# Cosine-similarity attention on one core: the orders of all five engines searched anew, the first scores ahead of the second pair's norm sums, its log among the first exponentials

## The chip, the cores and the metric

The kernel runs on one core of a Trainium2 chip. The program gives each of a core's five engines its own instruction list, and the lists meet only at semaphores: PE (TensorE, matrix multiply; PEld is its loading of weights), ACT (ScalarE), DVE (VectorE), POOL (GpSimd) and SP, which here only issues DMAs. A second list of DMA issues, shown as ACTq, stands on ACT. In these traces an instruction that waits holds up all behind it in its list.

The metric is the device time of one execution in microseconds (us), the median over several runs. The profile is of one execution; its span is about 2 us shorter than the device time. Some executions of a kernel are slower than the rest; a run over 1.5% above the fastest of its kernel is called slow here.

## The reference

```python
# Q, K, V: (8, 12, 512, 64) float32; tau = 0.1
Q_norm = Q / (np.linalg.norm(Q, axis=-1, keepdims=True) + 1e-10)
K_norm = K / (np.linalg.norm(K, axis=-1, keepdims=True) + 1e-10)
scores = np.einsum('bhqd,bhkd->bhqk', Q_norm, K_norm) / tau
weights = np.exp(scores - np.max(scores, axis=-1, keepdims=True))
weights = weights / (np.sum(weights, axis=-1, keepdims=True) + 1e-10)
return np.einsum('bhqk,bhkd->bhqd', weights, V).astype(np.float32)
```

## The kernel before

The 96 heads are worked off as 48 pairs, numbered 0 to 47. The program is a list of named operations with their needs, and a table `ORDER` that gives the order on each engine. The names, with s the pair and w = 0 for Q, 1 for K:

| name | engine | what |
|---|---|---|
| `LD.s.w`, `LV.s`, `ST.s` | SP (three of the K loads: ACT) | load Q or K, load V, store the result |
| `SQ` | POOL, for the first pairs also ACT | squares of Q and K |
| `SSQ.s`, `RED.s.0` | PE, DVE | sums of squares: a matmul against the identity, then a small reduction |
| `LN`, `EX` | ACT | for pairs 0 and 1: norms by a log and an exp |
| `NEW.g.k` | DVE | for later pairs, in groups: norms by an integer first guess and two Newton steps |
| `SCL.s.w` | DVE (Q), POOL (K) | scale by the norms |
| `TR.s`, `EVA.s` | PE, DVE | transpose, copy the transpose out of PSUM, the memory PE writes to |
| `XT.s` | SP | for seven of the pairs K is transposed by a DMA instead |
| `SCO.s.c`, `EXP.s.c` | PE, ACT | scores and exponentials of the c-th quarter, 128 keys of both heads (pair 0: one head at a time, 512 wide) |
| `VC`, `PV`, `RCP`, `NRM` | POOL, PE, DVE | V to bf16, weighted sums, normalization |
| `warm`, `fill` | PE | dummy matmuls that keep PE's clock up in the head |

How an order becomes waits, and the operations that the argument touches (cuts are marked `...`):

```python
for e, ops in order.items():
    for o in ops:
        o.waits = [self.ops[n] for n in o.needs]
        if e in ("pe", "act"):       # needs on the same engine: no wait
            o.waits = [p for p in o.waits if p.eng != e or p.slot is not None or p.key in o.hard]
...
# pair s: loads; K of pairs 0, 1 and 2 is issued from ACT's queue
for w, x in ((0, Q), (1, K)):
    P.add(("LD", s, w), "act" if w and s < 3 else "sp", [...],
          lambda e, w=w, x=x: e.dma_start(out=qk[iq][:, w], in_=src(x, s)), ...)
...
# exponentials: two banks of scores, so SCO.c waits for EXP.(c-2)
P.add(("EXP", s, c), "act", before, lambda e, c=c, b=b: e.activation(
    out=et[iet][:, c, :, :], in_=sc_ps[:, 2 * b : 2 * b + 2, :], func=ACT.Exp, scale=inv_tau))
...
XT = {33, 39, 9, 45, 15, 21, 27}
FILL = (9, 16)
ORDER = {
    "sp": """ LD.0.0.0 LD.0.0.1 LD.1.0 LD.2.0 LV.0 LD.3.1 LD.3.0 LD.4.1 LD.4.0 LD.5.1 LD.5.0 ... """,
    "act": """ table LD.0.1 LD.1.1 LD.2.1 SQ.0.0.1 SQ.0.1 LN.0.0 EX.0.0 LN.0.1 SQ.1.1 EX.0.1 SQ.2.1
               LN.1 EX.1.0 EX.1.1 EXP.0.0.0 EXP.0.0.1 EXP.0.1.0 ... """,
    ...
```

## Time and profile before

| | before |
|---|---|
| device time, median of 3 runs | 194.69 us (194.19 to 194.87) |
| span of the profiled run | 192.28 us |
| first exponential starts | 9.59 us |
| start of the last exponential to the end | 4.88 us |
| median start-to-start of the 1024-wide exponentials | 0.904 us |
| starts later than 0.904 us after the one before, summed | 3.3 us |

The last two rows are worked out from the start times of the exponentials in the trace.

ACT is busy for 95% of the span and its exponentials follow one another with hardly any idle time. (Neighbours overlap, so the mean of 1135 ns is longer than their spacing.) What can shrink is what comes before the first exponential, gaps in their stream, and what follows the last. The head of ACT's timeline (start us, duration us, engine, line, operation, output<-input, count, [idle before <-what ended it]):

```profile
1.33 1.01 ACTq L379 DMA_DIRECT2D qk<-in_K_dram  x2
...
5.53 0.18 ACT L263 ACTIVATE ops<-xl 128x8 f32<-128x8 f32 x1
6.07 0.21 ACT L259 ACTIVATE xl<-xs 128x8 f32<-128x8 f32 x1 [0.36 <-DVE xs L304]
6.19 0.61 ACT L229 ACTIVATE sq<-qk 128x512 bf16<-128x512 f32 x1
6.71 0.19 ACT L263 ACTIVATE xr<-xl 128x8 f32<-128x8 f32 x1
7.38 0.63 ACT L229 ACTIVATE sq<-qk 128x512 bf16<-128x512 f32 x1 [0.49 <-DMA qk<-in_K_dram]
9.12 0.21 ACT L259 ACTIVATE xl<-xs 128x16 f32<-128x16 f32 x1 [1.11 <-DVE xs L253]
9.37 0.18 ACT L263 ACTIVATE ops<-xl 128x8 f32<-128x8 f32 x1
9.49 0.19 ACT L263 ACTIVATE xr<-xl 128x8 f32<-128x8 f32 x1
9.59 4.76 ACT L443 ACTIVATE et<-scps,xr 128x512 bf16<-128x512 f32 x8
14.21 6.77 ACT L453 ACTIVATE et<-scps 128x1024 bf16<-128x1024 f32 x7
```

The two loads at 1.33 are K of pairs 1 and 2. The square at 7.38 is `SQ.2.1`, of pair 2's K; it starts as that load lands, at 7.36. Then ACT idles 1.11 us for pair 1's norm sum, does pair 1's log and two exps (9.12 to 9.59), and only then begins pair 0's exponentials.

### The profile page before, as it was taken

The numbers are of one execution on the slowest core, as the hardware profiler recorded it, in microseconds if no ns is written. First come the engines' busy times: TensorE is split into PE (matmuls) and PEld (weight loads), VectorE is DVE, ScalarE is ACT, GpSimd is POOL, SyncE is SP. The second block draws the span as 40 slices with busy tenths as digits, with TensorE's granted clock in tenths as the row PEclk, the third lists the DMA queues.
The fourth block names the chain that finished last, engine by engine and source line by source line (L and its number), as shares of the span: only waits on it lengthen the run. The fifth ranks groups of instructions, "written<-read, shape, count | busy, mean of one in ns | idle before, by whom it ended". The sixth has DMA issues, their size and how long they took to land.

```text
span 192.3 us, 7111 instructions
## 1 busy us (share of the span) xinstructions
PE 179.5 (93%) x2944; PEld 117.6 (61%) x2944; DVE 148.3 (77%) x450; ACT 182.3 (95%) x210; POOL 161.8 (84%) x149
## 2 busy tenths in 40 slices
PE   7799999999998999999999899999999999999891
PEld 5466666656665565666666565666566656566560
DVE  1588887988888798868897887798888778976632
ACT  3599999999999999999999999999999999999990
POOL 4599899999999969999989988799999999927000
PEclk9999999999999999999999999999999999999998
DMA  5999999999999999989999999038799536650545
GB/s 185 360 349 349 352 336 321 373 251 344 341 376 303 374 364 332 314 251 310 364 346 339 285 376 387 16 88 254 242 254 356 130 109 197 193 136 3 182 148 165
DMA packets 56240, 51.71 MB, mean 269 GB/s; under 512 B 6928, under 2 KB 56208, under 8 KB 56208
## 3 DMA queue, kind: packets, MB, share of 16 engines
q1 hardware_dynamic: 55248, 50.41, 84.6%
q10 hardware_dynamic: 960, 0.85, 1.3%
q8 instruction: 23, 0.38, 0.9%
q14 instruction: 9, 0.07, 0.1%
HBM read 37.75 MB, written 12.58 MB: 262 GB/s over the span
## 4 chain that ended last, share of the span: by engine, by line
ACT 67%; POOL 15%; PE 8%; DMA 3%; DVE 2%; issue 2%; SPq 0%
ACT et L453 67%; POOL sq L231 8%; POOL qn L270 4%; DMA qk<-in_Q_dram 3%; POOL vb L458 3%; PE scps L431 2%; PE ops L469 2%; PE xps L246 2%; PE ops L218 1%; PE xps L277 1%; DVE ob L513 1%; PE nps L498 0%; SPq L294 0%; DVE ob L483 0%; POOL vb L212 0%
## 5 line engine op out<-in xcount | busy, mean ns | idle before, releaser
L453 ACT ACTIVATE et<-scps 128x1024 bf16<-128x1024 f32 x187 | 172.2, 1135 | 0.3
L231 POOL TENSOR_TENSOR sq<-qk 128x1024 bf16<-128x1024 f32 (+2 forms) x48 | 87.5, 1837 | 4.2 <-DMA qk<-in_Q_dram 4.2
L431 PE MATMUL scps<-qt 64*128 64x512 bf16 x384 | 74.7, 386 | 4.4 <-ACT et L453 2.4
L469 PEld LDWEIGHTS ops<-vb,et 128*128 128x128 bf16 x1504 | 53.4, 98 | 27.2 <-issue 22.2
L469 PE MATMUL ops<-vb,et 128*128 128x65 bf16 x1504 | 68.2, 194 | 0.6 <-DVE nps L341 0.4
L270 POOL TENSOR_TENSOR qn<-qk,rk 128x512 bf16<-128x512 f32 x44 | 45.6, 1046 | 10.2 <-DVE rk L346 10.2
L421 DVE COPY qt<-xps 128x1024 bf16<-128x1024 bf16 (+1 forms) x47 | 30.4, 647 | 3.7 <-PE xps L277 3.2
L483 DVE TENSOR_TENSOR ob<-ops,rd 128x512 f32<-128x512 f32 x47 | 32.4, 689 | 1.1
L270 DVE TENSOR_TENSOR qn<-qk,nps 128x512 bf16<-128x512 f32 x48 | 31.9, 680 | 0.3
L431 PEld LDWEIGHTS scps<-qt 64*128 64x128 bf16 x384 | 18.6, 92 | 20.3 <-ACT et L453 7.4
L458 POOL TENSOR_SCALAR vb<-vf 128x512 bf16<-128x512 f32 x48 | 29.7, 630 | 0.0
L277 PE MATMUL xps<-ident,qn 128*128 128x128 bf16 x352 | 27.9, 220 | 0.4 <-DVE qn L270 0.2
L246 PE MATMUL xps<-sq,ident 128*128 128x64 bf16 x624 | 24.9, 192 | 2.0 <-POOL sq L231 0.9
L277 PEld LDWEIGHTS xps<-ident,qn 128*128 128x128 bf16 x352 | 19.9, 98 | 10.4 <-issue 3.0
L246 PEld LDWEIGHTS xps<-sq,ident 128*128 128x128 bf16 x624 | 20.8, 97 | 8.9 <-issue 3.8
L481 DVE RECIPROCAL rd<-ops 128x8 f32<-128x8 f32 x47 | 9.7, 206 | 15.6 <-PE ops L469 15.2
L253 DVE TENSOR_REDUCE nps<-xps 128x16 f32<-128x64 f32 x38 | 8.8, 232 | 9.3 <-PE xps L246 8.9
L240 DVE TENSOR_REDUCE nps<-sq 128x8 f32<-128x512 bf16 x16 | 10.8, 684 | 0.0
L341 DVE TENSOR_TENSOR nps<-nps,ys 128x32 f32<-128x32 f32 (+1 forms) x48 | 9.3, 195 | 1.1
L342 DVE SCALAR_TENSOR_TENSOR nps<-nps,ys 128x32 f32<-128x32 f32 (+1 forms) x48 | 9.2, 193 | 1.0
L218 PE MATMUL scps<-warm_in 128*128 128x256 bf16 x28 | 5.8, 384 | 1.1 <-DVE warm_in L216 1.1
L218 PEld LDWEIGHTS scps<-warm_in 128*128 128x128 bf16 x28 | 3.7, 138 | 2.3 <-DVE warm_in L216 1.1
(42 smaller groups left out, 46.1 us busy)
## 6 DMA issues: line engine op xcount, KB each, us to landing
vf<-in_V_dram SPq DMA_DIRECT2D x48, 256.0 KB, 6.0
qk<-in_Q_dram SPq DMA_DIRECT2D x47, 256.0 KB, 6.0
out_dram<-ob SPq DMA_DIRECT2D x47, 256.0 KB, 5.3
qk<-in_K_dram SPq DMA_DIRECT2D x45, 256.0 KB, 6.0
qk<-in_K_dram ACTq DMA_DIRECT2D x3, 256.0 KB, 4.7
qk<-in_Q_dram SPq DMA_DIRECT2D x2, 128.0 KB, 2.7
out_dram<-ob SPq DMA_DIRECT2D x1, 128.0 KB, 2.3
qt<-qn SPq DMA_TRANSPOSE x7, 4.9
```

The source lines that it names most:

```text
L218: P.add(key, "pe", needs, lambda e: e.matmul(out=bank[:, 0:256], lhsT=warm_in[:, 0:128], rhs=warm_in[:, :], start=True, stop=True))
L231: emit = lambda e: e.tensor_tensor(out=b, in0=a, in1=a, op=ALU.mult)
L240: lambda e, w=w: e.tensor_reduce(out=dst(w), in_=sq[s % R_SQ][:, 8 * w : 8 * w + 8, :], axis=AX.X, op=ALU.add))
L246: last = e.matmul(out=x_ps[:, 0:64], lhsT=ident[:, :], rhs=sq[s % R_SQ][:, :, 4 * k : 4 * k + 4], start=(k == 0), stop=(k == 15))
L270: lambda e: e.tensor_tensor(out=qn[iqn][:, w].rearrange("p t h d -> p h t d"), in0=qk[iq][:, w].rearrange("p h (t d) -> p h t d", t=NT), i ...
L277: last = e.transpose(dst[:, i, :], qn[s % R_QN][:, b // NT, b % NT].rearrange("p h d -> p (h d)"), ident[:, :])
L421: lambda e: e.tensor_copy(out=qt[iqt][:, :].rearrange("p w t x -> p (w t) x")[:, 0:nb], in_=tb[:, 0:nb]))
L431: last = e.matmul(out=sc_ps[:, 2 * b + h, :], lhsT=qt[iqt][64 * h : 64 * h + 64, 1, c, :], rhs=qt[iqt][64 * h : 64 * h + 64, 0, :, :], sta ...
L453: lambda e, c=c, b=b: e.activation(out=et[iet][:, c, :, :], in_=sc_ps[:, 2 * b : 2 * b + 2, :], func=ACT.Exp, scale=inv_tau))
L458: lambda e: e.tensor_scalar(out=vb[:, iq, :, :, 0:DIM].rearrange("p c h d -> p h c d"), in0=vf[iv][:, :, :].rearrange("p h (c d) -> p h c ...
L469: last = e.matmul(out=o_ps[:, h, 65 * t : 65 * t + 65], lhsT=et[iet][:, c, h, 128 * t : 128 * t + 128], rhs=vb[:, iq, c, h, :], start=(c = ...
L483: lambda e: e.tensor_tensor(out=ob[io][:, :], in0=grid[:, :, :, 0:DIM], in1=rd[io][:, :].unsqueeze(3).to_broadcast([128, 2, NT, DIM]), op= ...
```

## The change

The intent: let pair 0's scores and first exponentials go ahead of pair 1's norm work, and find better orders for the rest by a search in an event model whose durations were fitted to the chip. No operation is added or taken away; the lists of all five engines are permuted. The diff, cut to what bears on the argument:

```diff
-        dummy(("fill", k), *((sc_ps[:, 3], ["wz"]) if k < FILL[0] else (o_ps[:, 0], [("EVA", 0, 1)])))
+        low = k < FILL[0]
+        dummy(("fill", k), sc_ps[:, 3] if low else o_ps[:, 0],
+              [("fill", k - 1) if k else ("warm", WARM - 1), "wz" if low else ("EVA", 0, 1)])
+    P.ops["SCO", 0, 1].needs.append(("fill", FILL[0] - 1))
+    P.ops["PV", 0, 0, 0].needs.append(("fill", sum(FILL) - 1))
 ...
     "pool":
-        one eye SQ.0.0.0 SCL.0.1 SQ.1.0 vone SQ.2.0 SCL.1.1 VC.0 SQ.3.0 ...
+        one eye SQ.0.0.0 SCL.0.1 vone SQ.1.0 SQ.2.0 VC.0 SCL.1.1 SQ.3.0 ...
     "dve":
-        wz RED.0.0.0 RED.0.0.1 RED.0.1 SCL.0.0 EVA.0 EVA.0.1 RED.1.0 SCL.1.0 ...
+        wz RED.0.0.0 RED.0.0.1 EVA.0.1 SCL.0.0 RED.0.1 EVA.0 RED.1.0 SCL.1.0 ...
     "pe":
-        warm.0 ... warm.18 fill.0 TR.0.1 fill.1 ... fill.4 TR.0 fill.5 ... fill.8 SSQ.1
-        SCO.0.0 SCO.0.1 SSQ.2 fill.9 ... fill.15 TR.1 SCO.0.2 ...
+        warm.0 ... warm.18 fill.0 ... fill.5 TR.0.1 fill.6 ... fill.11 TR.0 fill.12 fill.13
+        SCO.0.0 SCO.0.1 SSQ.1 fill.14 ... fill.18 SSQ.2 fill.19 SCO.0.2 TR.1 ...
     "act":
-        table LD.0.1 LD.1.1 LD.2.1 SQ.0.0.1 SQ.0.1 LN.0.0 EX.0.0 LN.0.1 SQ.1.1 EX.0.1 SQ.2.1 LN.1 EX.1.0 EX.1.1
-        EXP.0.0.0 EXP.0.0.1 EXP.0.1.0 ...
+        LD.0.1 LD.1.1 table SQ.0.0.1 SQ.0.1 LN.0.0 EX.0.0 LD.2.1 SQ.1.1 LN.0.1 EX.0.1 SQ.2.1 EXP.0.0.0 EXP.0.0.1 LN.1
+        EX.1.1 EX.1.0 EXP.0.1.0 ...
```

`LD.2.1`, the load of pair 2's K, moves from third place in ACT's list to behind the first small exp, `EX.0.0`.

## The prediction

> **What bounds the kernel now.** ScalarE's stream of exponentials. The chain of waits gives ACT 67%, and from 61.0 to 184.0 us it is 134 exponentials in 123.08 us with nothing between. In the timeline the exponentials run from 9.59 us (eight 512-wide ones, 0.57 us apart) to 187.82 us. The median start-to-start of the 1024-wide ones is 0.904 us. The Trainium skill ("ScalarE: Activation LUTs", section "What ACT_TABLE_LOAD costs") gives 0.833 ns per element, so 853 ns for 1024; the trace agrees but for 51 ns, so only three things can shrink: the 9.59 us before the first one, gaps in the stream, and the 4.46 us after the last (last normalization, store, landing). Starts more than 0.904 us apart sum to 3.3 us of gaps, in some 22 places, worst 1.18 to 1.21 us for 0.90; there TensorE brings the next scores late. POOL (84%) and DVE (77%) are not the limit.
>
> **What the change does.** The same instructions in other orders. (The new needs of the dummy matmuls tie PE to PE and DVE values already awaited, so they emit no wait.)
>
> *Head.* Before: second pair's norm matmuls, its sum, its log (9.12), two exps, first exponential 9.59; ScalarE stood idle 1.1 us (waits: xl after xs). After: first scores go ahead, and the log and two small exps (together 0.46 us) come after two exponentials. But other moves cost time. Six dummies stand before K's transposes (there was one): about 0.9 us, K transposed at 6.6 for 6.0. DVE takes K's eviction (0.42) before scaling Q (0.68) and before K's norm sum (0.69), so that sum ends near 8.3 (was 6.04). Then log, exp, the square of pair 2 (0.5): first exponential near 9.2. That pair's K load is now issued from ScalarE's queue only after the first exp, about 5.6 for 1.85; the three such loads before took 3.2 to 5.5 us, so it lands near 8.4 to 8.9, another possible hold. Estimate: first exponential 9.2 (9.0 to 9.6), third 10.8 (was 10.73). The head is worth about zero, where the intent says half a microsecond. Second pair's scaling starts 1.1 us later (10.8 for 9.71); I expect small gaps at pairs 1 to 3 (0.3 to 0.8 us in all).
>
> *Middle.* Between consecutive scores PE now has more even work. Counting the order with durations from the trace (scores 0.325, transposes 0.45, norm sums 0.47, weighted-sum group 0.117), intervals over 1.0 us fall from 15 to 4. I expect the gaps after pair 3 to fall from about 2.9 to about 1.5 us; waits on POOL and DVE for those inputs remain.
>
> *Tail.* The last stores only swap order: 0 to 0.1 us.
>
> **Predicted time: 193.8 us**, 8-in-10 range 192.2 to 195.5. Over 2% faster needs 3.9 us, more than all gaps. Chances: faster 0.03, same 0.93, slower 0.04.
>
> **What would show it.** Timeline, ACT: first exponential near 9.2, log inside the 512-wide ones, first 1024-wide one at 14.1 to 14.5 (was 14.21). DVE: K's eviction ahead of Q's scaling, ending near 7.1. Exponentials of the middle: mean spacing falling from 0.923 towards 0.913. Span from last exponential to end: 4.4 to 4.5.
>
> **What would make it wrong.** The clock of PE rising earlier or later than near 6.0 us; pair 2's K load landing late (over 9 us: head loses 0.3 to 0.5 us more); a squares or scaling order on POOL that now stalls PE in the middle (gaps stay or grow); or the late second pair pushing a longer bubble through pairs 1 to 4.

## More of the kernel before

The page of the kernel before, its engine line, the row of PE's granted clock (40 slices of the span, in tenths of full speed), the chain of work that ended last, and the exponentials' group (count | busy us, mean ns | idle before):

```profile
PE 179.5 (93%) x2944; PEld 117.6 (61%) x2944; DVE 148.3 (77%) x450; ACT 182.3 (95%) x210; POOL 161.8 (84%) x149
...
PEclk9999999999999999999999999999999999999998
...
ACT 67%; POOL 15%; PE 8%; DMA 3%; DVE 2%; issue 2%; SPq 0%
...
L453 ACT ACTIVATE et<-scps 128x1024 bf16<-128x1024 f32 x187 | 172.2, 1135 | 0.3
```

## The result, and the profile after

| | before | after |
|---|---|---|
| device time, median | 194.44 us (4 runs, 193.73 to 194.87) | 199.37 us (4 runs, 198.17 to 199.74) |
| ratio of the fast runs | | 1.0245 (95% interval 1.0208 to 1.0281) |

The four runs of the kernel before lie within 0.6% of each other. A ratio here and below is the mean time of one kernel's fast runs over that of the other's in the same rounds, so not quite the ratio of the medians. The change made the kernel 2.5% slower.

The page of the kernel after, the same lines:

```profile
PE 181.8 (92%) x2944; PEld 118.0 (60%) x2944; DVE 144.9 (73%) x450; ACT 182.6 (92%) x210; POOL 161.9 (82%) x149
...
PEclk9985999999999999999999999999999999999999
...
ACT 71%; PE 14%; DMA 8%; DVE 1%; issue 1%; POOL 1%; SPq 1%; DVEq 0%
...
L453 ACT ACTIVATE et<-scps 128x1024 bf16<-128x1024 f32 x187 | 172.2, 1205 | 2.1 <-PE scps L431 2.0
```

The same work, busy as long as before (172.2 us of exponentials in both), in a longer span. Two things are new: a dip in PE's granted clock in the third and fourth slice (about 10 to 20 us), and DMA in the chain with 8% instead of 3%. ACT's timeline, after:

```profile
1.30 0.49 ACTq L379 DMA_DIRECT2D qk<-in_K_dram  x1
...
5.40 0.18 ACT L263 ACTIVATE ops<-xl 128x8 f32<-128x8 f32 x1
5.41 0.37 ACTq L379 DMA_DIRECT2D qk<-in_K_dram  x1
5.83 0.63 ACT L229 ACTIVATE sq<-qk 128x512 bf16<-128x512 f32 x1 [0.25 <-DMA qk<-in_K_dram]
8.34 0.21 ACT L259 ACTIVATE xl<-xs 128x8 f32<-128x8 f32 x1 [1.88 <-DVE xs L304]
8.57 0.21 ACT L263 ACTIVATE xr<-xl 128x8 f32<-128x8 f32 x1
12.45 0.63 ACT L229 ACTIVATE sq<-qk 128x512 bf16<-128x512 f32 x1 [3.67 <-DMA qk<-in_K_dram]
12.99 1.25 ACT L443 ACTIVATE et<-scps,xr 128x512 bf16<-128x512 f32 x2
14.13 0.21 ACT L259 ACTIVATE xl<-xs 128x16 f32<-128x16 f32 x1
...
17.45 1.27 ACT L443 ACTIVATE et<-scps,xr 128x512 bf16<-128x512 f32 x2 [0.46 <-PE scps L431]
18.74 1.02 ACT L453 ACTIVATE et<-scps 128x1024 bf16<-128x1024 f32 x1
```

The load issued at 5.41 is `LD.2.1`. ACT reaches `SQ.2.1` at 8.8 and stands for 3.67 us until that load lands, with all of pair 0's exponentials behind it. The pieces of the chain of waits around it (start, length, what):

```profile
5.40 0.01 ACT ops L263
5.41 7.02 DMA qk<-in_K_dram
12.43 0.02 issue
12.45 0.02 ACT sq L229
12.48 0.51 issue
12.99 1.25 ACT et L443 x2
```

The load took 7.02 us from issue to landing, against 5.51 us for the same load issued at 1.85 before the change.

### The profile page after: what moved, and what is told of

Same layout as the page of the kernel before. It is cut to its first block, busy times and chain, and to the rows that moved or that the text cites. A ratio compares the mean times of both kernels' runs of the same rounds, so it can differ in the third digit from the quotient of the medians.

```text
span 198.0 us, 7087 instructions
## 1 busy us (share of the span) xinstructions
PE 181.8 (92%) x2944; PEld 118.0 (60%) x2944; DVE 144.9 (73%) x450; ACT 182.6 (92%) x210; POOL 161.9 (82%) x149
## 4 chain that ended last, share of the span: by engine, by line
ACT 71%; PE 14%; DMA 8%; DVE 1%; issue 1%; POOL 1%; SPq 1%; DVEq 0%
ACT et L453 70%; PE scps L431 5%; PE ops L469 4%; DMA qk<-in_K_dram 4%; DMA out_dram<-ob 3%; PE xps L277 2%; PE xps L246 2%; DMA qk<-in_Q_dram 2%; POOL sq L231 1%; SPq L487 1%; ACT et L443 1%; PE ops L218 1%; DVE ob L513 0%; ACT sq L229 0%; DVE ob L483 0%
## 5 line engine op out<-in xcount | busy, mean ns | idle before, releaser
L453 ACT ACTIVATE et<-scps 128x1024 bf16<-128x1024 f32 x187 | 172.2, 1205 | 2.1 <-PE scps L431 2.0
L469 PE MATMUL ops<-vb,et 128*128 128x65 bf16 x1504 | 67.3, 194 | 1.4 <-issue 1.0
L246 PE MATMUL xps<-sq,ident 128*128 128x64 bf16 x624 | 25.7, 194 | 2.8 <-ACT sq L229 2.8
L246 PEld LDWEIGHTS xps<-sq,ident 128*128 128x128 bf16 x624 | 21.3, 98 | 10.5 <-issue 7.3
L229 ACT ACTIVATE sq<-qk 128x512 bf16<-128x512 f32 (+1 forms) x4 | 2.2, 572 | 5.1 <-DMA qk<-in_K_dram 3.9
```

Of the source, the lines that this page charges most:

```text
L246: last = e.matmul(out=x_ps[:, 0:64], lhsT=ident[:, :], rhs=sq[s % R_SQ][:, :, 4 * k : 4 * k + 4], start=(k == 0), stop=(k == 15))
L453: lambda e, c=c, b=b: e.activation(out=et[iet][:, c, :, :], in_=sc_ps[:, 2 * b : 2 * b + 2, :], func=ACT.Exp, scale=inv_tau))
L469: last = e.matmul(out=o_ps[:, h, 65 * t : 65 * t + 65], lhsT=et[iet][:, c, h, 128 * t : 128 * t + 128], rhs=vb[:, iq, c, h, :], start=(c = ...
```

## The experiments

Theory A: nearly all the loss comes of one token, `LD.2.1`, whose late issue puts it behind SP's loads; ACT's list, in order, carries its lateness into every exponential. Rival B: the rest of the new orders costs the time (K's transposes six dummies later, DMA transposes and stores placed otherwise), and the late load only coincides. All experiment kernels gave correct results. Each was timed against the kernel before in the same rounds. The rounds ran on four chips, so compare the ratios; a trace is of one execution only.

### 1. The change with the K load issued early

```diff
 "act":
-  LD.0.1 LD.1.1 table SQ.0.0.1 SQ.0.1 LN.0.0 EX.0.0 LD.2.1 SQ.1.1 ...
+  LD.0.1 LD.1.1 LD.2.1 table SQ.0.0.1 SQ.0.1 LN.0.0 EX.0.0 SQ.1.1 ...
```

> The changed kernel with one token moved back: pair 2's K load is issued third on ScalarE's queue, ahead of the table load, instead of after the first small exp. Theory A (late K load is the cause): it lands near 7.4 us instead of 12.43, the first exponential starts near 9.2 us instead of 12.99, PE keeps its full clock through 14 to 19 us, and the time falls by 4 to 6 us, to 194 to 195.5. Rival B (the other moves of the head and the new orders of SP and PE in the middle are the cause): the first exponential moves but the time stays over 197.

Measured: 194.24 us (6 runs, 193.32 to 194.86), before 194.06; ratio 1.0003 (0.9973 to 1.0034). ACT's timeline of this version:

```profile
1.30 1.01 ACTq L379 DMA_DIRECT2D qk<-in_K_dram  x2
...
8.91 0.61 ACT L229 ACTIVATE sq<-qk 128x512 bf16<-128x512 f32 x1
9.43 1.25 ACT L443 ACTIVATE et<-scps,xr 128x512 bf16<-128x512 f32 x2
...
14.44 5.86 ACT L453 ACTIVATE et<-scps 128x1024 bf16<-128x1024 f32 x6
```

One token takes the whole loss away. The load landed at 7.83. All the other moves of the change together neither gain nor lose: rival B falls for the loss, and what remains to explain is why they gain nothing.

### 2. The kernel before with the K load issued late

```diff
 "act":
-  table LD.0.1 LD.1.1 LD.2.1 SQ.0.0.1 SQ.0.1 LN.0.0 EX.0.0 LN.0.1 ...
+  table LD.0.1 LD.1.1 SQ.0.0.1 SQ.0.1 LN.0.0 EX.0.0 LD.2.1 LN.0.1 ...
```

> The kernel before with the same one token moved the other way: pair 2's K load issued after the first small exp on ScalarE's queue. Theory A: it lands near 12 us (before: 7.36), the first exponential starts near 12.5 to 13.7 us (before: 9.59) and the time rises by 3 to 6 us, to 197.5 to 200.5. Rival B: under 1 us more.

Measured: 198.90 us (4 runs, 198.22 to 199.37), ratio 1.0244 (1.0206 to 1.0281). The load, issued at 5.42, landed at 12.19 and the first exponential began at 13.19:

```profile
5.42 0.38 ACTq L379 DMA_DIRECT2D qk<-in_K_dram  x1
...
12.21 0.63 ACT L229 ACTIVATE sq<-qk 128x512 bf16<-128x512 f32 x1 [5.42 <-DMA qk<-in_K_dram]
...
13.19 2.40 ACT L443 ACTIVATE et<-scps,xr 128x512 bf16<-128x512 f32 x4
```

The one token alone makes the old kernel as much slower as the whole change did (1.0245).

### 3. What the late load waits for

The load itself is 256 KB; why does it take 7 us? Theory A1: loads from both queues are served in the order in which they were issued, so it stands behind SP's backlog. Rival A2: a late load on ACT's queue is slow in itself, or loses against later ones. The change, with one wait added that keeps SP's loads back until `EX.0.0`:

```diff
+    P.ops["LV", 0].needs.append(("EX", 0, 0))
```

> The changed kernel with one wait added: SP's loads from the first V on wait for the first small exp (about 5.6 us), so that the late K load (issued at 5.4) has no backlog of SP loads ahead of it but the same competition after it. Theory A1 (loads of the two queues are served in order of issue, so what it waits for is the seven or so loads issued before it): it takes 2.7 to 3.5 us from issue to landing, lands at 8.1 to 9.0, first exponential at 9.1 to 9.6, time 194.5 to 197 (the held loads may cost something later). Rival A2 (a load on ScalarE's queue issued late is slow whatever stands ahead, or loses to SP's loads issued after it): it still takes about 7 us and the first exponential starts near 13 us.

Measured: the load was issued at 5.43, as before, and landed at 8.16, after 2.73 us. Time 194.47 us (4 runs, 194.19 to 195.62), ratio 1.0038 (0.9996 to 1.008). ACT's timeline:

```profile
5.43 0.37 ACTq L379 DMA_DIRECT2D qk<-in_K_dram  x1
...
8.37 0.62 ACT L229 ACTIVATE sq<-qk 128x512 bf16<-128x512 f32 x1
8.89 1.25 ACT L443 ACTIVATE et<-scps,xr 128x512 bf16<-128x512 f32 x2
```

The late issue is harmless when little stands ahead, although SP's loads follow from 5.63 on. The first exponential, at 8.89, came even earlier than expected. A2 falls.

### 4. The load at a place between

```diff
 "act":
-  LD.0.1 LD.1.1 table SQ.0.0.1 SQ.0.1 LN.0.0 EX.0.0 LD.2.1 SQ.1.1 ...
+  LD.0.1 LD.1.1 table SQ.0.0.1 LD.2.1 SQ.0.1 LN.0.0 EX.0.0 SQ.1.1 ...
```

> The changed kernel with the K load issued after the first square on ScalarE's queue, about 4.3 us: between 1.82 (landed 7.83) and 5.41 (landed 12.43). Theory A1 (served in order of issue, about 0.75 us for each load ahead): it stands behind the load SP issued at 3.72, which landed at 9.56, and beside the one of 4.23, which landed at 10.26, so it lands at 10.0 to 10.9, the first exponential starts at 10.6 to 11.6, time 196 to 197.5. Rival A2 (late on that queue is slow in itself): it lands about 7 us after issue, 11.2 or later, or in about 3 us, 7.5.

Measured: issued at 4.36, landed at 11.27, first exponential at 11.83, time 197.94 us (4 runs), ratio 1.0182 (1.0164 to 1.02). The landing is 0.4 us later than my range and so within what I had given the rival; run 3 has excluded that rival, and the order of landings says the same. Issue and landing of the loads around it, read from the two traces (times in us, the K load in bold):

| load, change as it is | issued | landed | load, K load at 4.36 | issued | landed |
|---|---|---|---|---|---|
| SP, K of pair 3 | 3.21 | 8.43 | SP, K of pair 3 | 3.21 | 8.23 |
| SP, Q of pair 3 | 3.72 | 9.56 | SP, Q of pair 3 | 3.72 | 9.48 |
| SP, K of pair 4 | 4.23 | 10.26 | SP, K of pair 4 | 4.23 | 10.53 |
| SP, Q of pair 4 | 5.11 | 11.60 | **ACT, K of pair 2** | **4.36** | **11.27** |
| **ACT, K of pair 2** | **5.41** | **12.43** | SP, Q of pair 4 | 4.80 | 11.73 |
| SP, K of pair 5 | 5.62 | 12.20 | SP, K of pair 5 | 5.31 | 12.04 |
| SP, Q of pair 5 | 6.44 | 13.32 | SP, Q of pair 5 | 6.00 | 13.25 |

Across both queues the loads land in order of issue, but for one pair of neighbours 0.2 us apart. SP issues a load about every 0.5 us and one lands about every 0.75 us, so the time from issue to landing grows: 2.3 us for the first (half as large as the others), 6.5 for the one at 5.11. The Trainium skill ("DMA: Bandwidth & Descriptors", section "Issuing engines are not separate DMA queues") says that DMAs of all issuing engines run on the same 16 DMA engines and interleave; these traces agree, and show that a second queue is no way past the backlog of the first.

This run shows a second thing. Its first exponential began 1.16 us earlier than the change's (12.99), yet pair 4 began only 0.09 us earlier (30.84 instead of 30.93): PE's granted clock was at a half from 14.11 to 20.93 here too (the next but one run takes that apart). Of the 1.34 us between the two profiled spans, 1.27 lie from pair 4 on, where the two kernels' orders are the same.

### 5. Loads late, but what hangs on them out of the way

Does the lateness hurt because it stands in ACT's list ahead of work that doesn't need it? The change with the load left late:

```diff
 "act":  SQ.2.1 from ahead of EXP.0.0.0 to behind EXP.0.2.0
 "pe":   SSQ.2 from behind fill.18 to behind SCO.0.3
 "dve":  EVA.1 ahead of RED.2.0;  EVA.2 ahead of NEW.1.0
```

> The changed kernel with its late K load left late, but what hangs on it moved behind pair 0's exponentials: the square of pair 2's K after the fifth 512-wide exponential on ScalarE, pair 2's norm sum after pair 0's scores on PE, the evictions of pairs 1 and 2 ahead of pair 2's and group 1's norm arithmetic on DVE. Theory A (the late load hurts because every queue is served in order and the square stands ahead of the first exponential): first exponential near 9.2 us instead of 12.99, PE stays warm, pair 2 starts 1 to 2 us later than before the change (19 to 20 us), time 195 to 197. Rival C (pair 2's data is needed so early that its lateness costs the same wherever it is awaited): time stays within 1 us of the changed kernel, 198.4 or more.

Measured: 196.24 us (4 runs, one of them slow), ratio of the fast ones 1.0087 (1.0054 to 1.012). The load landed at 12.23, the first exponential began at 9.39, and pair 2's at 20.47 instead of 23.36. Pair 2 came later than I had expected (19 to 20). More than half of the loss goes. Of what is left, 1.75 us show as one gap, ahead of pair 1's third exponential: on PE pair 2's transposes (`TR.2`) stand ahead of its score, so the late pair still holds up work that doesn't need it. Rival C falls, theory A stands.

### 6. The lowered clock

After the change PE idles from 10.42 (its last dummy) to 13.18, for the norm sum of pair 2. The trace has its granted clock at a half from 12.90 to 19.73. The change with 26 more dummies in that stretch:

```diff
-FILL = (9, 16)
+FILL = (9, 42)
 "pe":  fill.25 to fill.50 put in behind fill.18
```

> The changed kernel with 26 more dummy matmuls on PE while it waits for pair 2's norm sum, from 10.3 to about 13.1 us, so that its clock is not lowered. The late load is untouched, so the first exponential stays near 13 us. If the lowered clock is what made pairs 0 to 2 lose a further 1.4 us (first exponential to pair 2: 10.37 us against 8.92 with the early load): the granted clock stays 1.0, scores take 0.39 us again instead of 0.60, and the time falls by 0.7 to 1.5 us, 197.8 to 198.6. If those gaps are the late norm arithmetic alone: within 0.4 us of 199.37.

Measured: 197.84 us (4 runs, 197.48 to 198.13), ratio 1.0177 (1.0131 to 1.0222) where the change had 1.0245 (1.0208 to 1.0281). The two intervals just overlap; what decides is the stretch in the traces. Two stretches of the head by windows (length, busy us (instructions) of each engine, granted clock, DMA share, GB/s), first of the change:

```profile
10.00:14.00 4.00, 1.24 (x20) 0.97 (x19) 0.13 (x1) 1.55 (x3) 0.00 (x0) 0.86 1.10 350
14.00:20.00 6.00, 5.10 (x41) 2.48 (x39) 4.27 (x15) 5.25 (x11) 5.34 (x4) 0.52 1.10 348
```

and with the dummies:

```profile
10.00:14.00 4.00, 3.58 (x45) 2.86 (x43) 0.00 (x0) 1.85 (x4) 0.00 (x0) 1.00 1.10 349
14.00:20.00 6.00, 4.80 (x65) 2.94 (x65) 5.12 (x18) 5.85 (x12) 5.63 (x4) 1.00 1.10 348
```

With the clock at 1.00, PE gets through 65 matmuls in the six microseconds, and without it 41 in more busy time. The first exponential stays late (12.69), but from there to pair 4 it takes 16.50 us, as with the early load (16.49), against 17.94 in the change.

With this the loss can be added up from the start times of the exponentials in the profiled runs of the change and of run 1 (K load early), which differ by 5.57 us in span:

| stretch | change | K load early | difference |
|---|---|---|---|
| to the first exponential | 12.99 | 9.43 | +3.56: waiting for the K load |
| first exponential to pair 4 | 17.94 | 16.49 | +1.44: the lowered clock (gone in run 6) |
| pair 4 to the last exponential | 162.46 | 161.82 | +0.63: gaps in the middle, unlike from version to version though the orders there are the same (section 8) |
| last exponential to the end | 4.63 | 4.70 | -0.07 |

### 7. The stated idea by itself

The kernel before, with the first scores ahead of pair 1's norm sum and its log among the exponentials, the K load early:

```diff
 "pe":   ... fill.8 -SSQ.1- SCO.0.0 SCO.0.1 +SSQ.1+ SSQ.2 +SCO.0.2+ fill.9 ... TR.1 +SCO.0.3+ ...
 "act":  ... SQ.2.1 -LN.1 EX.1.0 EX.1.1- EXP.0.0.0 EXP.0.0.1 +LN.1 EX.1.1 EX.1.0+ EXP.0.1.0 ...
```

> The kernel before with the stated idea alone: pair 0's first two scores ahead of pair 1's norm sums on PE (and the third ahead of the dummies, the fourth ahead of two), and pair 1's log and two small exps after the first two exponentials on ScalarE; nothing else moved, the K load stays early. If the idea is sound: first exponential near 8.3 us (before: 9.59), third near 9.9 (before: 10.73), and up to 0.8 us less time, 193.5 to 194.2. If the idea itself costs: gaps of over 1 us at pairs 0 to 2 and the same time or more.

Measured: 194.21 us (6 runs), ratio 1.0014 (0.9986 to 1.0042): the same. The exponentials do start earlier and then lose it (starts in us):

| | first | third | pair 1 | pair 2 |
|---|---|---|---|---|
| before | 9.59 | 10.73 | 14.21 | 17.83 |
| idea alone | 8.72 | 10.32 | 13.91 | 17.91 |

The later log makes pair 1's K scaling on POOL start at 10.39 instead of 9.76, POOL's squares of pair 3 at 11.99 instead of 11.36, and PE, which has pair 3's norm sum ahead of pair 1's second score, brings that score late: the gap after pair 1's first exponential is 0.36 us. The gain is given back two pairs on, where POOL and PE set the pace. That is read from the one trace; I made no run to take POOL's part away. Nor is all of the early start the idea's: PE's clock rose at 5.60 us here and at 6.08 before, and the kernel of the last run below, whose head is that of the kernel before, began at 9.94 where the clock rose at 6.83.

### 8. Why the middle gained nothing

From pair 4 on, the starts that come more than 0.904 us after the one before sum to 2.88 us before the change and to 2.97 us in run 1, where I had expected about 1.5. One trace says little about so small a sum: the change and runs 1, 3, 4, 5 and 6 have the same orders from pair 4 on, and their sums are 3.52, 2.97, 3.32, 2.24, 3.20 and 3.00. Run 1 has large gaps at two places: 0.91 us ahead of pair 15 and 0.52 us inside pair 29. At pair 15 the DMA transpose `XT.15` landed at 66.41 for an exponential that began at 66.88; before the change it landed 2 us ahead of its exponential. The gap in pair 29 I put down to the buffer of an earlier store, from the chain of the change: it runs there through a store of 5.43 us into DVE's normalization. Four versions tried to mend the middle:

```diff
 run a, on run 1:  "pool": SCL.15.1 ahead of SQ.18.0, SCL.27.1 ahead of VC.27
                   "sp":   ST.17 ST.20 ST.21 ahead of XT.27
 run b, on run 1:  as a, without the move of SCL.27.1
 run c:            as b, and XT = {33, 39, 9, 45, 15, 21} (pair 27's K by PE)
 run d, on run 1:  XT = {33, 39, 9, 45, 15, 21} alone
```

Run a:

> The version with the early K load (194.24 us), with the two scalings of pairs 15 and 27 one or two places earlier on POOL and three stores ahead of a DMA transpose on SP. Theory D (what kept the middle from gaining is that DMA transposes and stores now end just as they are needed: pairs 15 or 27 and 29 lost 0.9 and 0.5 us there): those gaps shrink to under 0.3 us and the time falls by 0.7 to 1.4 us, 192.8 to 193.6. Rival E (the gaps wander to the next late transfer): within 0.4 us of 194.2.

Measured 195.72 us (6 runs), ratio 1.0077 (1.0046 to 1.0108). Pair 29's gap went and pair 15's halved to 0.49, but POOL, waiting for the scales of pair 27, delayed a norm sum (1.72 us lost in pair 24), and pair 27 lost 0.81 us. The gaps wander as the rival said, but the time lies outside both ranges.

Run b:

> The version with the early K load (194.24 us), with the scaling of pair 15 alone one place earlier on POOL (not that of pair 27, whose move made POOL wait and cost 1.7 us at pair 24) and the three stores ahead of a transpose on SP. Theory D (late transposes and stores are what kept the middle from gaining): pair 15's gap falls under 0.5 us, pair 29's (0.52 us) goes, nothing new opens, 193.0 to 193.9. Rival E (each order is tuned as a whole, and a gap closed in one place opens in another): 194.0 or more.

Measured 194.44 to 199.47 us; three of six runs count as slow, the fast three have a ratio of 1.0069 (0.9986 to 1.0152). My edit had a fault: the stores that I put ahead of `XT.27` wait for their own data and take SP's time, so the transpose was issued later still, at 106.93 instead of 104.19 in run 1. Pair 29's gap went, pair 15's fell only to 0.70. The profile shows what a late one costs, in the chain of waits:

```profile
106.24 0.69 DVE ob L483
106.93 6.30 DMA qt<-qn
113.23 0.04 issue
113.27 0.41 PE scps L431 x2
```

The transpose, 6.30 us from where SP takes it up to its landing, ends in the score that pair 27's first exponential needs; that exponential came 2.77 us late. The transfer itself was hardly slower than in run 1 (6.05 us). The answer is the rival's.

Run c:

> The same with pair 27's K transposed on PE instead of by DMA (four more transposes, an eviction of 1024 for 512 columns). If the late DMA transpose of pair 27 still costs 0.2 to 0.8 us, this takes it away: 0.2 to 0.6 us under the run before it, 192.8 to 193.6. Rival: the added 0.2 us on PE and 0.3 us on DVE come at the same tight place and nothing is gained.

Measured 192.39 us (6 runs, 191.81 to 193.43), ratio 0.9907 (0.9865 to 0.9948): the only version faster than both kernels, by 0.9% against the kernel before, and below my range. Its gaps from pair 4 on sum to 2.09 us, none over 0.12; run 4 has 2.24 with none of these edits. The exponentials of its page and the chain:

```profile
ACT 87%; PE 8%; DVE 2%; issue 0%
...
L453 ACT ACTIVATE et<-scps 128x1024 bf16<-128x1024 f32 x187 | 171.9, 1248 | 0.2
```

Run d, to part this gain:

> The changed kernel with the early K load and pair 27's DMA transpose replaced by PE's, and nothing else: the store order and the order on POOL are the change's own. It parts the run of 192.39 us in two. Theory F (the one DMA transpose is what it gained by: it also stands in SP's in-order queue waiting for POOL, and holds up the stores behind it): 192.0 to 193.2, no gap at pairs 27 and 29. Rival G (moving three stores and the scaling of pair 15 is what gained): 193.6 to 194.4, with gaps of about 0.9 us at pair 15 and 0.5 us at pair 29 left.

Measured 193.90 us (6 runs), ratio 0.9982 (0.9944 to 1.0021). Gaps of 0.72 us at pair 15, 0.40 in pair 27 and 0.30 in pair 29 stay. By the times it is neither edit alone: the moved stores and scaling lose or gain nothing in run b (1.0069), the transpose alone gains nothing here, and both together have 0.9907. That the stores gain only once the transpose no longer stands behind them on SP would explain it, but it is not shown. The intervals of c and d meet (0.9948 and 0.9944), the two were timed on different chips, and of the 1.53 us between their profiled spans 1.02 lie ahead of the first exponential, where their orders are the same and PE's clock rose at 4.51 us in c and at 7.12 in d.

A last run asked whether the kernel before could be mended on PE alone, by putting a score ahead of the norm sum or weighted-sum group before it in 14 places with gaps:

```diff
 "pe":  ... PV.0.1.3 -SSQ.5- SCO.2.1 +SSQ.5+ TR.3 ...      (and 13 more such swaps, one past four groups)
```

> The kernel before with PE alone changed: in 14 places the next score goes ahead of the norm sum or of one weighted-sum group that stood before it. If the gaps of the exponentials in the middle are PE bringing scores late in those places, 1.0 to 1.8 of the 2.9 us after pair 4 go and the time is 192.4 to 193.4. If POOL and DVE set the pace there (the norm sums wait for squares), the gaps move to other places and the time stays at 193.8 to 194.6.

Measured 196.01 us (6 runs, 195.22 to 197.43), ratio 1.0097 (1.007 to 1.0124): slower by 1%, outside both ranges. The gaps from pair 4 on grew to 4.03 us and moved to other places. My reading is that a norm sum that yields its place comes late to DVE and POOL, and that their lateness returns as larger gaps; no run shows this by itself.

One version could not run: with POOL's and SP's old lists and the other new ones the waits of the table form a circle (POOL stops at `SCL.32.1`, SP at `XT.33`). That follows from the tables alone.

## Why the prediction was wrong

- **The bound was right.** ACT's exponentials set the time; their busy time did not change (172.2 us in both).
- **The step that failed is one term of the head:** "the three such loads before took 3.2 to 5.5 us, so it lands near 8.4 to 8.9, another possible hold". It took 7.02 us and landed at 12.43. I took the size from loads issued in the first two microseconds, when little stood ahead. The loads that SP issued at about 5.4 in the kernel before were the ones to look at: the one issued at 5.17 landed at 11.87, after 6.7 us, in the very trace I had. Its arithmetic was there too: nine loads issued before 5.4 had not landed by then in that trace; with the K load itself that makes ten, and at about 0.75 us each an estimate of 7.5 us.
- **The warning was right and its size was wrong.** I named "pair 2's K load landing late (over 9 us: head loses 0.3 to 0.5 us more)". It lost 3.56 us, and the lowered clock 1.44 us more, a consequence I had not thought of at all.
- **The rest of the head was right.** K's eviction ended at 7.11 (predicted 7.1), K's norm sum at 8.30 (8.3). With the early load the first exponential came at 9.43 (9.2), the third at 11.03 (10.8); that the first fell within 9.0 to 9.6 owes something to luck, since five versions with this head and the early load began anywhere from 8.48 to 9.62, with PE's clock (below). The gaps of pairs 1 to 3 were 0.64 us (0.3 to 0.8).
- **The middle was wrong as well.** "I expect the gaps after pair 3 to fall from about 2.9 to about 1.5 us": with the early load they stayed at 2.97. Counting PE's work between scores left out what the new orders did to DMA transposes, one of which ended the largest gap (pair 15). Run c, with edits to transposes and stores, has 2.09; but with sums of 2.24 to 3.52 over versions that share one order, why the middle gained nothing stays open.
- **The tail** was 0.25 us shorter from the start of the last exponential, where I had given 0 to 0.1.

Open: why the middle gained nothing, which part of run c's gain is its own and which is the phase of PE's clock (below), and why run 7's early gain could not be kept.

## What to carry to other kernels

Cost a moved load by the backlog at its new moment of issue, not by what that load took before: here another engine's queue did not get past it. In a list served in order, put nothing that waits for a late transfer ahead of work that doesn't need it, and ask whether PE will idle long enough to lose its clock (2.76 us were enough in the change). Orders tuned together break apart when one is changed: 14 plausible swaps on PE alone cost 1%.

## What the Trainium skill lacked or had wrong

- "DMA: Bandwidth & Descriptors", section "Queues, rings and completion order": it says that each DMA engine takes turns between the queue rows that have work. Here a load on ACT's row, issued at 5.41 with SP's row backed up, had its first packets only at 8.60 and landed at 12.43, about in order of issue; with SP held back its first packets came at 6.46, and it landed 2.73 us after issue. The page does say that the two rows have no DMA engine or descriptor generator of their own, but not that the backlog of one holds up a load on the other, nor how the time to landing grows with it (3.1 to 8 us for loads of 256 KB issued within the first 10 us).
- "TensorE: Matmul & The Clock Gate", section "What's actually happening": it gives the low clock "after ≥1 idle window (~3.4µs)". Here PE did not have to be idle for all of such a window. In the three traces where the clock fell early (the change, runs 2 and 4), it fell 6.83, 6.83 and 10.24 us after its rise, two or three times 3.41 us, and PE had been busy for 0.93, 0.94 and 1.13 of the 3.41 us just before; in run 4 it had been busy for 1.75 of the 3.41 us before those, and kept its clock. Nor does the length of the idle stretch give the moment: in run 4 PE idled from 9.34 to 12.02, worked, and idled again from 13.52; the clock fell at 14.11. It stayed low for 6.83 us each time.
- The same section says that the window is free-running, so that the start of the full clock varies by ±500 ns. Here it varies from 3.87 to 7.12 us over the fourteen profiled runs, in all of which the first matmul starts at 1.12 us. That is as large as the effects sought in sections 7 and 8: with the six dummies ahead of K's transposes and the early load, the first exponential began at 8.48 or 8.60 us where the clock rose at 4.58 or 4.51, at 9.29 where it rose at 6.25, and at 9.43 or 9.62 where it rose at 6.53 or 7.12.
- "ScalarE: Activation LUTs", section "What ACT_TABLE_LOAD costs": 186 ns + 0.833 ns per element (for immediate scale and bias) less 93 ns of overlap gives, as an estimate from that page, 946 ns between 1024-wide exponentials; the trace has 904, 42 less.
- No page has what a DMA transpose from SBUF to SBUF costs among other traffic: 4.9 us from issue to landing in the median of the seven in the kernel before (2.47 to 6.26), and up to 7.39 in the change.
